# The down-projection of a two-layer decoder: eight groups of blocks in place of nine, the last bank copied ahead of the SiLU, other pages for the first group's operands

## The chip, the cores and the metric

The kernel runs on one core of one Trainium2 chip. The metric is the device time of one execution in microseconds (us); the time before is the median of three runs.

Five engines have queues of their own, and each runs its queue in order. TensorE (PE in the profile) multiplies matrices into PSUM. VectorE (DVE), ScalarE (ACT) and GpSimd (POOL) compute element by element. SyncE (SP) issues the DMA transfers between HBM and the on-chip memory SBUF. An instruction that waits holds back all that stand behind it in its own queue.

## The reference

Two layers, each a token mixer and then a feed-forward block (the ConvFFN), both followed by a LayerNorm over a scaled residual. The change lies in the feed-forward block of both layers (1024 tokens, width 1024, FFN_DIM 2816, that is 22 blocks of 128 channels):

```
def conv_ffn(h, w_up, b_up, conv_w, conv_b, w_down, b_down):
    up = causal_dwconv(h @ w_up + b_up, conv_w, conv_b)
    g, val = jnp.split(up, 2, axis=-1)
    return (jax.nn.silu(g) * val) @ w_down + b_down

# in each layer, with sh2, sc2, g2 worked out from the conditioning vector c
h = x * (1.0 + sc2) + sh2
y = conv_ffn(h, w_up[l], b_up[l], conv_f_w[l], conv_f_b[l], w_down[l], b_down[l])
x = layer_norm(DEEPNORM_ALPHA * x + (1.0 + g2) * y, ln_g[l, 1], ln_b[l, 1])
```

Everything is float32.

## The kernel before

**Products in three parts.** A float32 operand is split into a rounded high part (ScalarE's cast, L125) and the rest as a low part (a subtraction, L126). A product is three matmuls: high by high, high by low, low by high (L130 to L132 in the down-projection, L1092 to L1094 in the up-projection). Tiles of SBUF are "pages" of 128 partitions; a page can be written again when its last reader is done.

**Up-projection (`up_phase`).** One iteration for each of the 22 blocks of channels, and one more to finish. The seven products of a Strassen-like scheme go into PSUM banks called `upa`, `upb` and `upd`, are summed on VectorE (L1116), pass through the three-tap convolution (a ScalarE activation, L1125, and VectorE's L1129) into tiles `cv`, and through the SiLU (L1211). The finished block goes to memory as `d_act` (L1177). The value half of a block is convolved one iteration later than its gate half: the bank that the last product (number 4, into `upb`) fills is copied to `upc` by ScalarE at the head of the next iteration (L1151). TensorE, ScalarE and VectorE run this function in the order in which it is written.

**Down-projection (`ffn`, from L1244).** The 22 blocks are taken in groups of `sizes`, 2, 3, 3, 3, 3, 2, 2, 1, 3. For each block of a group `load_act` loads the activations from `d_act` (tile `actr`) and splits them, and `load_wdown` loads the rows of the weights (tile `wdn`), multiplies them by the gate row (L1240) and splits them. The parts go to pages named `dn`; `sets` are two sets of such pages that the groups use in turn, and the first group has a choice of its own: `ya`, pages of the up-projection's operand `A`, and `xc`.

Then `out_group` (L892) makes eight token tiles of 128 by 1024. Each gathers 6 n matmuls for n blocks in two banks of PSUM (tile `og`; there are three such pairs, and two more single banks, in place of the up-projection's eight). In the first group ScalarE copies the pair to the sum `r` (L903); in each later group VectorE adds it (L905).

**Work beside it.** After each group `pump` lets a few steps of two generators into the program. One (only in layer 0) works out the next layer's modulation: loads of `wada`, VectorE's L260. The other, `residual_in` (L1024), adds the residual to `r`: it loads two rows of parameters (`agab`), then for each of eight token tiles a tile `xr` of the residual (two buffers), multiplies it (L1034), adds (L1035) and adds it to `r` (L1036). What is left is done ahead of the last group's products.

At the end of layer 0 the last group goes through `boundary`: each token tile gets its LayerNorm (VectorE's L352, L354, L137, GpSimd's L138, VectorE's L363); then each half of the tokens is transposed on TensorE (L333, tile `tr`), taken out of PSUM by ScalarE (L340, L343) and VectorE (L346) as the next layer's operand `h`, from which the next projection (`prj`) starts. Beside it weights of the next layer are split (ScalarE's cast to `vwh`, GpSimd's subtraction to `vwl`). In front of the transposes TensorE has the matmuls of the modulation (`modp`, L269, and `gatet`, L286).

Outside `up_phase` a scheduler orders the instructions of each engine by estimated times and priorities, so a change of group sizes moves instructions at many places.

Of the kernel before, what the change touches and what calls it, by code (L numbers as in the profile page):

```python
# [13 lines left out]
F32R = mybir.dt.float32r  # L14
# [6 lines left out]
P = 128  # L21
D = 1024
S = 1024
L = 2
# [26 lines left out]
class Trunk:  # L51
# [1044 lines left out]
    def up_phase(self, l, H, A):  # L1096
        nc = self.nc
        act, v = nc.scalar, nc.vector
# [5 lines left out]
        cg, cv = self.page("Ra", "upc"), self.page("Ra", "upc")  # L1104
# [13 lines left out]
        def cast(n, src):  # L1118
            act.copy(self.up_w[n][:, 0], src)  # L1119

        def sub(n, src):
            tt(self.up_w[n][:, 1], src, self.up_w[n][:, 0].bitcast(F32), ALU.subtract)

        def lin(m, c, u):
            act.activation(out=u, in_=c, func=AF.Identity, bias=self.ffcc[:, m:m + 1], scale=self.ffw[:, 2, m:m + 1])  # L1125
# [7 lines left out]
        b, d = self.bank("upb"), self.bank("upd")  # L1133
# [4 lines left out]
        for f in range(NF + 1):  # L1138
            run, nxt = f < NF, f + 1 < NF
# [8 lines left out]
                a = self.bank("upa")  # L1148
                self.product(a, H, 2)
            if f:  # L1150
                act.copy(cv[:, 0:512], pb)  # L1151
                lin(NF + f - 1, cv, uv)
                if run:
                    cast(4, o22)
# [49 lines left out]
            taps(f, cg, ug)  # L1204
            self.product(b, H, 4, True)
            pb = b
            if nxt:
                b = nb
                act.copy(e1, b)
                sub(7, n21)  # L1210
# [33 lines left out]
    def ffn(self, l, H, A, O):  # L1244
        nc = self.nc
        self.ffn_cols(l)
        self.psum(0, 8)
        with self.tc.manual_schedule(engines={nc.tensor.engine, nc.scalar.engine, nc.vector.engine}):
            self.up_phase(l, H, A)
        self.psum(3, 2)  # L1250
        pages = lambda tag, n: [self.page(tag, "dn", F32R) for _ in range(n)]
        ya, xc = pages(A + "a", 8), pages(O + "c", 4)
        xa = []
        for _ in range(2):
            t = self.page(O + "a", "dn", F32R, (P, 4, 1024))
            xa += [t[:, i] for i in range(4)]
        yb, yc = pages(A + "b", 4), pages(A + "c", 4)
        sets = [(ya[:6], yc + ya[6:]), (xa[:6], xa[6:] + yb)]
        grow = self.gate_row(l, 1)
        r = {}  # L1260
        f0 = 0
        sizes = (2, 3, 3, 3, 3, 2, 2, 1, 3)
        for j, n in enumerate(sizes):
            last = j == len(sizes) - 1
            acts, wts = (ya[:4], xc) if j == 0 else sets[j % 2]
            lhs = [self.load_act(l, f0 + i, acts[2 * i], acts[2 * i + 1]) for i in range(n)]
            w = [self.load_wdown(l, f0 + i, wts[2 * i], wts[2 * i + 1], grow) for i in range(n)]
            f0 += n
            if j == 0:
                for t in (4, 5, 6, 7, 0, 1, 2, 3):  # L1270
                    r[t] = self.page("Ra" if t < 4 else "Rb", "r")
                self.out_group(lhs, w, r, None, (4, 5, 6, 7, 0, 1, 2, 3), True)
                self.bg.append(self.residual_in(l, r, O))
                if l + 1 < L:
                    self.mod_tile = [self.page(O + "c", "wada") for _ in range(3)] + [self.page(O + "c", "macc")]
                self.pump(2)
            elif not last:
                self.out_group(lhs, w, r)
                self.pump(3 * n + 2 if l + 1 < L else 2)
            else:  # L1280
                self.drain_bg()
                if l + 1 < L:
                    for ww in range(2):
                        self.affine_cols(l + 1, ww)
                    pre = self.za_first(l + 1, A)
                    Hn = self.boundary(l, 1, lhs, w, r, O)
                    self.bg.append(self.residual(l, r, "tmp"))
                    return Hn, pre
                self.final_rows(l, lhs, w, r)
# [143 lines left out]
```

## Time and profile before

| | us |
|---|---|
| median of three runs | 2542.33 |
| lowest and highest | 2537.85, 2546.43 |
| the profiled execution | 2538.86 |
| its span in the trace | 2537.2 |
| TensorE busy | 2354.1 (93%) |
| VectorE busy | 2066.2 (81%) |
| ScalarE busy | 1066.0 (42%) |
| GpSimd busy | 395.1 (16%) |

The profiled execution lies within the runs' range; its mean granted TensorE clock is 0.959 of full speed (2.4 GHz; 0.50 is 1.2 GHz). Times in the rows are us from the start of the span. In layer 0 the passage from up- to down-projection lies at 1000 to 1045 us and the down-projection ends at 1302; in layer 1 the passage lies at 2255 to 2297 and the down-projection ends at 2518. Busy shares are averages over stages with different limits, so each place is read by itself: first what TensorE waits for there, then what the engine named was doing.

### The profile page before, as it was taken

The page shows a single profiled execution, that of the slowest core. Times are in us where ns is not written, and L with a number is a line of the kernel's source. Part 1 is how long each engine was busy: PE and PEld are TensorE (multiplying, and loading weights), DVE is VectorE, ACT ScalarE, POOL GpSimd, SP SyncE. Part 2 cuts the span into 40 slices and gives each one's busy share as a digit, 9 for nine tenths or more (in the row PEclk, how much of TensorE's full clock was granted, in tenths as well). Part 3 has the DMA queues.
Part 4 walks back from the last instruction along what each step waited for, and adds up shares of the span by engine and source line. Part 5 has one row for each costly group of instructions (what it writes and reads, how often), then busy time and mean ns, then how long its engine had stood idle before and what let it go on. Part 6 is the DMA issues. An engine that isn't in the chain of part 4 may idle for free. (4 is left out here: it accounts for less than half of the span.)

```text
span 2537.2 us, 28532 instructions
## 1 busy us (share of the span) xinstructions
PE 2354.1 (93%) x10846; PEld 1912.6 (75%) x10846; DVE 2066.2 (81%) x2794; ACT 1066.0 (42%) x1708; POOL 395.1 (16%) x213
## 2 busy tenths in 40 slices
PE   8999989988999999999789999999899999989996
PEld 7777768766888887788578776777678888868885
DVE  7998787889887888778979987768887777797768
ACT  4314744645554554311131157445554554552111
POOL 1243160433000000000020542213510000000003
PEclk9998979999999999999889998999899999999998
DMA  8443433222332334645513244220322222254311
GB/s 295 152 153 130 160 142 117 75 100 71 112 110 90 117 108 155 206 142 182 172 61 133 87 160 164 95 108 32 108 75 83 84 83 83 84 183 148 100 42 67
DMA packets 88826, 302.47 MB, mean 119 GB/s; under 512 B 9392, under 2 KB 18928, under 8 KB 87152
## 3 DMA queue, kind: packets, MB, share of 16 engines
q1 hardware_dynamic: 88688, 300.65, 34.9%
q8 instruction: 85, 1.39, 0.2%
q14 instruction: 53, 0.43, 0.1%
HBM read 232.42 MB, written 68.19 MB: 118 GB/s over the span
## 5 line engine op out<-in xcount | busy, mean ns | idle before, releaser
L130 PE MATMUL og<-dn,dn 128*128 128x512 f32 x704 | 281.2, 399 | 37.6 <-DVE r L905 21.6
L1092 PE MATMUL upb<-comb,uw 128*128 128x512 f32 x704 | 275.9, 392 | 10.9 <-DVE upc L1116 6.7
L131 PE MATMUL og<-dn,dn 128*128 128x512 f32 x704 | 278.5, 396 | 0.0
L132 PE MATMUL og<-dn,dn 128*128 128x512 f32 x704 | 278.3, 395 | 0.0
L1093 PE MATMUL upb<-comb,uw 128*128 128x512 f32 x704 | 275.4, 391 | 2.7 <-DVE comb L980 2.7
L1094 PE MATMUL upb<-comb,uw 128*128 128x512 f32 x704 | 274.9, 391 | 0.0
L1116 DVE TENSOR_TENSOR uw<-wu,uw 128x512 fp32r<-128x512 f32 x210 | 144.2, 687 | 125.3 <-ACT uw L1119 125.3
L138 POOL TENSOR_TENSOR lnrs<-lnrs,mhalf 128x1 f32<-128x1 f32 x32 | 20.8, 653 | 1386.1 <-DVE lnrs L137 1374.4
L905 DVE TENSOR_TENSOR r<-og,r 128x1024 f32<-128x1024 f32 x144 | 174.6, 1219 | 66.8 <-PE og L132 66.0
L1129 DVE SCALAR_TENSOR_TENSOR cv<-upc,pc,cv 128x1023 f32<-128x1023 f32 (+1 forms) x176 | 225.4, 1281 | 2.8
L130 PEld LDWEIGHTS og<-dn,dn 128*128 128x128 f32 x704 | 134.5, 191 | 72.1 <-DVE r L905 27.2
L410 DVE SCALAR_TENSOR_TENSOR convacc<-convy,pc,convacc 128x1023 f32<-128x1023 f32 (+14 forms) x120 | 178.7, 1489 | 1.8
L125 ACT CAST dn<-actr 128x1024 fp32r<-128x1024 f32 x44 | 46.0, 1049 | 306.5 <-PE og L131 146.2
L1092 PEld LDWEIGHTS upb<-comb,uw 128*128 128x128 f32 x704 | 132.7, 188 | 41.6 <-DVE upc L1116 8.4
L1119 ACT CAST uw<-wu 128x512 fp32r<-128x512 f32 x210 | 121.7, 616 | 83.6 <-DVE wu L1116 77.1
L1093 PEld LDWEIGHTS upb<-comb,uw 128*128 128x128 f32 x704 | 132.8, 189 | 31.8 <-DVE comb L980 4.5
L132 PEld LDWEIGHTS og<-dn,dn 128*128 128x128 f32 x704 | 134.4, 191 | 28.2
L131 PEld LDWEIGHTS og<-dn,dn 128*128 128x128 f32 x704 | 134.8, 192 | 27.4
L1094 PEld LDWEIGHTS upb<-comb,uw 128*128 128x128 f32 x704 | 132.7, 189 | 27.6
L1093 PE MATMUL upd<-comb,uw 128*128 128x512 f32 x352 | 138.1, 392 | 5.9 <-DVE comb L980 5.9
L1092 PE MATMUL upd<-comb,uw 128*128 128x512 f32 x352 | 137.7, 391 | 0.0
L1094 PE MATMUL upd<-comb,uw 128*128 128x512 f32 x352 | 137.3, 390 | 0.0
(327 smaller groups left out, 5812.1 us busy)
## 6 DMA issues: line engine op xcount, KB each, us to landing
wada<-in_w_ada SPq DMA_DIRECT2D x96, 512.0 KB, 4.5
wu<-in_w_up_t SPq DMA_DIRECT2D x84, 512.0 KB, 3.6
d_act<-cv SPq DMA_DIRECT2D x44, 512.0 KB, 2.6
actr<-d_act SPq DMA_DIRECT2D x44, 512.0 KB, 4.2
wdn<-in_w_down SPq DMA_DIRECT2D x44, 512.0 KB, 4.2
win<-in_w_fm SPq DMA_DIRECT2D x24, 512.0 KB, 4.5
wtm<-in_w_tm SPq DMA_DIRECT2D x16, 512.0 KB, 3.7
d_v<-vhl SPq DMA_DIRECT2D x16, 512.0 KB, 2.9
```

What stands on the lines that cost most here:

```text
L125: nc.scalar.copy(hi, src)
L130: mm(ps, lh, rh, start=first, stop=False)
L131: mm(ps, lh, rl, start=False, stop=False)
L132: mm(ps, ll, rh, start=False, stop=last)
L410: nc.vector.scalar_tensor_tensor(out=acc[:, d:], in0=y[:, :S - d], scalar=w(30 - d), in1=acc[:, d:], op0=ALU.mult, op1=ALU.add)
L905: nc.vector.tensor_tensor(out=r[t], in0=ps, in1=r[t], op=ALU.add)
L1092: mm(ps, w[:, 0, ks], hi[k], start=k == 0 and not more, stop=False, skip_group_check=True)
L1093: mm(ps, w[:, 0, ks], lo[k], start=False, stop=False, skip_group_check=True)
L1094: mm(ps, w[:, 1, ks], hi[k], start=False, stop=k == 3, skip_group_check=True)
L1116: v.tensor_tensor(out=o, in0=x, in1=y, op=op)
L1119: act.copy(self.up_w[n][:, 0], src)
L1129: v.scalar_tensor_tensor(out=u[:, d:], in0=c[:, :S - d], scalar=self.ffw[:, 2 - d, m:m + 1], in1=u[:, d:], op0=ALU.mult, op1=ALU.add)
```

## The change

Four edits.

1. In the last up-projection iteration the copy of the last bank moves from the head of the finishing iteration to a place ahead of the SiLU (a new line, L1209, in place of L1151's last run).
2. The groups are 2, 3, 3, 3, 3, 3, 2, 3: eight in place of nine.
3. The first group's activations use two new pages (`xb`) that hold the up-projection's operands of products 5 and 6, and the second group takes the set with `ya`; the sets swap their turns.
4. In layer 0 `pump` lets in 3 n steps after a group of n blocks in place of 3 n + 2; in layer 1 nothing after the first group.

```
@@ up_phase
             if f:
-                act.copy(cv[:, 0:512], pb)
+                if run:
+                    act.copy(cv[:, 0:512], pb)
                 lin(NF + f - 1, cv, uv)
...
             self.product(b, H, 4, True)
             pb = b
+            if not nxt:
+                act.copy(cv[:, 0:512], pb)
             if nxt:
                 b = nb
                 act.copy(e1, b)
@@ ffn
-        sets = [(ya[:6], yc + ya[6:]), (xa[:6], xa[6:] + yb)]
+        xb = []
+        for _ in range(2):
+            t = self.page(O + "b", "dn", F32R, (P, 2, 1024))
+            xb += [t[:, i] for i in range(2)]
+        sets = [(xa[:6], xa[6:] + yb), (ya[:6], yc + ya[6:])]
...
-        sizes = (2, 3, 3, 3, 3, 2, 2, 1, 3)
+        sizes = (2, 3, 3, 3, 3, 3, 2, 3)
...
-            acts, wts = (ya[:4], xc) if j == 0 else sets[j % 2]
+            acts, wts = (xb, xc) if j == 0 else sets[j % 2]
...
-                self.pump(2)
+                    self.pump(2)
...
-                self.pump(3 * n + 2 if l + 1 < L else 2)
+                self.pump(3 * n if l + 1 < L else 2)
```

(The first `pump` moves into the branch for layer 0 by its indentation.)

Layer 0 has 55 background steps left at that point, 47 of the modulation and then 8 of the residual. Before, 2, 13, 24, 35, 46, 54 and 55 of them are in the program after each group, so that the residual is done ahead of the last two groups; now 2, 11, 20, 29, 38, 47 and 53, and the last two ahead of the last group.

Line numbers behind L1151 grow by one, behind L1209 by three, behind the sets by up to seven.

How the instructions move, at three places; `dn`, `actr`, `wdn`, `upc` and `og` are the tiles named above, with their buffer numbers.

ScalarE around the last copy of a bank, layer 1, before:

```order
L125 CAST dn_16524<-actr_16691 128x1024 [waits DMAHW0_49]
L125 CAST dn_16525<-actr_16695 128x1024 [waits DMAHW1_49]
L1211 ACTIVATE cv_13766<-cv_13766 128x1024 [waits DVE_49,Activation_49]
L1151 COPY upc_13764<-upb_16374 128x512 [waits PE_49]
L1125 ACTIVATE cv_13767<-upc_13764,ffcc_13744,pc_91 128x1024 [waits Activation_49]
L125 CAST dn_16530<-wdn_16894 128x1024 [waits DVE_49]
L125 CAST dn_16532<-wdn_16899 128x1024 [waits DVE_49]
L903 COPY r_16554<-og_16562 128x1024 [waits PE_49]
```

and now:

```order
L125 CAST dn_16500<-actr_16666 128x1024 [waits DMAHW5_49]
L125 CAST dn_16502<-actr_16670 128x1024 [waits DMAHW6_49]
L125 CAST dn_16504<-wdn_16684 128x1024
L1209 COPY upc_13750<-upb_16360 128x512 [waits PE_49,Activation_49]
L1214 ACTIVATE cv_13752<-cv_13752 128x1024 [waits DVE_49,Activation_49]
L1125 ACTIVATE cv_13753<-upc_13750,ffcc_13730,pc_91 128x1024 [waits Activation_49]
L125 CAST dn_16510<-actr_16862 128x1024 [waits DMAHW0_49]
L125 CAST dn_16511<-wdn_16874 128x1024
L125 CAST dn_16512<-wdn_16879 128x1024 [waits DVE_49]
L903 COPY r_16542<-og_16550 128x1024 [waits PE_49]
```

The copy now stands ahead of the SiLU, and one more cast of weights stands ahead of both; the first copy of `og` (L903) has a cast of a loaded `actr` in front of it.

VectorE around the add that frees the last product (`upc<-upe,upb`), layer 0, before:

```order
L1029 TENSOR_SCALAR agab_8855<-agab_8855 128x1024 [waits DMAHW4_49,PE_49]
L1116 TENSOR_TENSOR cv_4857<-cv_4857,cv_4859 128x1024 [waits DVE_49]
L1116 TENSOR_TENSOR upc_4855<-upe_4850,upd_7577 128x512 [waits PE_49,Activation_49]
L126 TENSOR_TENSOR dn_7677<-actr_7835,dn_7677 128x1024 [waits DMAHW6_49,Activation_49]
L1034 TENSOR_TENSOR xr_8856<-xr_8856,agab_8855 128x1024 [waits DMAHW7_49,DVE_49]
L1116 TENSOR_TENSOR upc_4856<-upe_4851,upb_7527 128x512 [waits PE_49]
L1034 TENSOR_TENSOR xr_8856<-xr_8856,agab_8855 128x1024 [waits DMAHW0_49]
L126 TENSOR_TENSOR dn_7678<-wdn_7847,dn_7678 128x1024 [waits Activation_49]
```

and now:

```order
L126 TENSOR_TENSOR dn_7687<-actr_7691,dn_7687 128x1024 [waits Activation_49]
L1116 TENSOR_TENSOR cv_4857<-cv_4857,cv_4859 128x1024 [waits DVE_49]
L126 TENSOR_TENSOR dn_7684<-wdn_7849,dn_7683 128x1024 [waits PE_49]
L126 TENSOR_TENSOR dn_7666<-actr_7837,dn_7665 128x1024 [waits DMAHW4_49,Activation_49]
L126 TENSOR_TENSOR dn_7688<-actr_7695,dn_7688 128x1024 [waits Activation_49]
L1116 TENSOR_TENSOR upc_4855<-upe_4850,upd_7577 128x512 [waits PE_49,Activation_49]
L1116 TENSOR_TENSOR upc_4856<-upe_4851,upb_7527 128x512 [waits PE_49]
L126 TENSOR_TENSOR dn_7686<-wdn_7854,dn_7685 128x1024 [waits Activation_49]
```

The residual's L1029 and L1034 are gone from here; four subtractions L126 stand ahead of the two bank adds.

TensorE at the end of layer 0's down-projection (`tr` are the transposes), before:

```order
L286 MATMUL gatet_8851<-ident,gatec_8691 16x128
L333 MATMUL tr_9268<-ident,r_7711 128x128
L333 MATMUL tr_9268<-ident,r_7712 128x128
L333 MATMUL tr_9268<-ident,r_7713 128x128
L132 MATMUL og_9369<-dn_7685,dn_7668 128x512
L130 MATMUL og_9369<-dn_7671,dn_7669 128x512
L131 MATMUL og_9369<-dn_7672,dn_7669 128x512
L333 MATMUL tr_9268<-ident,r_7714 128x128
L132 MATMUL og_9369<-dn_7671,dn_7670 128x512
```

and now:

```order
L132 MATMUL og_9413<-dn_7685,dn_7668 128x512
L130 MATMUL og_9413<-dn_7671,dn_7669 128x512
L131 MATMUL og_9413<-dn_7672,dn_7669 128x512
L132 MATMUL og_9413<-dn_7671,dn_7670 128x512
L269 MATMUL modp_8897<-ones,macc_7832 128x1 x8
L286 MATMUL gatet_8910<-ident,gatec_8693 16x128
L333 MATMUL tr_9254<-ident,r_7713 128x128
L333 MATMUL tr_9254<-ident,r_7714 128x128
L333 MATMUL tr_9254<-ident,r_7715 128x128
```

Before, transposes of the first token half lie among the last tiles' matmuls; now all of them follow the last tile, behind `gatet`. In VectorE's order between the last L905 of the fifth group and the last L363 there are now 25 L905 (33 before), 11 L126 (13), 2 L1240 (3), 17 L260 (16) and no L346 (7).

## Rows read from the trace of the kernel before

**Rows 1.** The page: busy us of each engine, share of the span, instructions.

```profile
PE 2354.1 (93%) x10846; PEld 1912.6 (75%) x10846; DVE 2066.2 (81%) x2794; ACT 1066.0 (42%) x1708; POOL 395.1 (16%) x213
```

**Rows 2.** TensorE's waits, 918 to 1320 us: us in total, times, longest.

```profile
PE og L130 <- DVE r L905: 19.7, 7, 9.9
PE upb L1092 <- DVE upc L1116: 4.7, 1, 4.7
PE og L130 <- ACT r L903: 4.2, 1, 4.2
...
PE tr L333 <- DVE r L363: 3.8, 2, 3.0
```

**Rows 3.** TensorE's waits, 2255 to 2500 us.

```profile
PE og L130 <- ACT upc L1151: 11.0, 1, 11.0
PE og L130 <- DVE r L905: 1.9, 3, 0.6
PE upb L1092 <- DVE upc L1116: 1.1, 1, 1.1
PE og L130 <- ACT r L903: 0.8, 1, 0.8
```

**Rows 4.** Windows: length, busy us (count) by engine, granted clock, DMA share, GB/s.

```profile
1010.00:1022.00 12.00, 11.39 (x38) 9.04 (x39) 12.00 (x12) 6.04 (x7) 0.00 (x0) 0.74 0.68 208
1024.50:1036.00 11.50, 7.28 (x24) 5.82 (x24) 9.36 (x13) 4.80 (x5) 0.00 (x0) 0.70 0.61 193
2274.70:2286.00 11.30, 11.22 (x40) 9.10 (x41) 10.41 (x11) 6.10 (x7) 0.00 (x0) 0.80 0.60 197
```

**Rows 5.** One window, tile og alone: layer 0's second group.

```profile
1044.80:1077.40 32.60, 32.60 (x145) 27.02 (x144) 8.49 (x7) 1.00 (x1) 1.00 0.63 214
```

**Rows 6.** VectorE's groups, 1181.5 to 1312.1 us: count, busy us, mean ns, idle.

```profile
L905 DVE TENSOR_TENSOR r<-og,r 128x1024 f32<-128x1024 f32 x33 | 40.0, 1219 | 1.5 <-PE og L132 1.4
...
L363 DVE TENSOR_SCALAR r<-r,lnmv,lnrs 128x1024 f32<-128x1024 f32 x8 | 10.1, 1263 | 1.0 <-POOL lnrs L138 0.9
```

**Rows 7.** ScalarE's timeline, layer 1: start, us, instruction, [idle before <- releaser].

```profile
2267.76 1.04 ACT L125 CAST dn<-actr 128x1024 fp32r<-128x1024 f32 x1 [1.75 <-DMA actr<-d_act]
2273.20 1.06 ACT L1211 ACTIVATE cv<-cv 128x1024 f32<-128x1024 f32 x1 [4.39 <-DVE cv L1116]
2274.16 0.57 ACT L1151 COPY upc<-upb 128x512 f32<-128x512 f32 x1
```

**Rows 8.** SyncE's queue (DMA issues), layer 1.

```profile
2261.59 1.73 SPq L1232 DMA_DIRECT2D actr<-d_act  x2
```

**Rows 9.** VectorE's timeline, layer 0.

```profile
1009.87 0.68 DVE L1116 TENSOR_TENSOR upc<-upe,upb 128x512 f32<-128x512 f32 x1
```

**Rows 10.** VectorE's timeline, layer 1.

```profile
2257.32 0.68 DVE L1116 TENSOR_TENSOR upc<-upe,upb 128x512 f32<-128x512 f32 x1
```

**Rows 11.** ScalarE's timeline, layer 0.

```profile
1006.52 1.04 ACT L125 CAST dn<-actr 128x1024 fp32r<-128x1024 f32 x1 [5.44 <-DMA actr<-d_act]
```

**Rows 12.** VectorE's timeline, the boundary of the layers.

```profile
1304.30 2.40 DVE L363 TENSOR_SCALAR r<-r,lnmv,lnrs 128x1024 f32<-128x1024 f32 x1
...
1309.16 2.92 DVE L363 TENSOR_SCALAR r<-r,lnmv,lnrs 128x1024 f32<-128x1024 f32 x1
```

**Rows 13.** ScalarE's timeline, the boundary: transposed banks taken out of PSUM.

```profile
1312.65 1.45 ACT L340 ACTIVATE hf<-tr,sh,sc 128x512 f32<-128x512 f32 x2 [1.97 <-PE tr L333]
...
1315.02 1.46 ACT L340 ACTIVATE hf<-tr,sh,sc 128x512 f32<-128x512 f32 x2
```

**Rows 14.** TensorE's timeline, the boundary: the next layer's first projection matmul.

```profile
1319.86 0.56 PE L130 MATMUL prj<-h,wh 128*128 128x512 f32 x1
```

**Rows 15.** GpSimd's timeline, the boundary.

```profile
1303.79 2.35 POOL L126 TENSOR_TENSOR vwl<-wtm,vwh 128x1024 fp32r<-128x1024 f32 x1
...
1309.19 5.10 POOL L126 TENSOR_TENSOR vwl<-wtm,vwh 128x1024 fp32r<-128x1024 f32 x2
```

**Rows 16.** Loads of tile xr, 1180 to 1310 us: issue to landing.

```profile
DMA to landing us min/median/max: 3.3/4.4/5.8
```

## The prediction

> **What bounds the kernel now.** I read the page first, then TensorE's waits in the two stretches that the change touches, then the clock there, then the timeline of the engine that each wait names, and last the groups of VectorE at the end of layer 0.
>
> TensorE is busy for 93% of the span [rows 1]. Only its idle time and its time at half clock can be had, and the question is how much of either lies in the two down-projections. The reader is to see three places.
>
> First, the passage from up- to down-projection. In layer 0 the last product waits 4.7 us for VectorE's add L1116 and the fourth output tile 4.2 us for ScalarE's copy L903 [rows 2]; in layer 1 the second output tile waits 11.0 us for the copy L1151, and 1.1 and 0.8 us are lost beside it [rows 3]. Each long wait has a price behind it: the mean granted clock is 0.74, 0.70 and 0.80 in the eleven or twelve us that follow, though TensorE is busy in nearly all of two of them [rows 4].
>
> Second, the end of layer 0's down-projection: seven waits for VectorE's add L905, 19.7 us, the longest 9.9, and 3.8 for its L363 [rows 2].
>
> Third, in layer 1 the group of one block: three waits for L905, 1.9 us [rows 3].
>
> Elsewhere in the down-projection TensorE is the bound: a group of three blocks has 144 matmuls and takes 32.6 us without a gap at full clock [rows 5], about 10.9 us a block. Its eight adds on VectorE need 8 x 1.22 = 9.8 us, however many blocks there are [rows 6]. A group of one block therefore leaves VectorE almost nothing for other work.
>
> **The change, part by part.** The profiled execution took 2538.9 us, the median of the three runs is 2542.3; gains are worked out in the first and taken off the second.
>
> *Copy of the last bank.* In layer 1 it starts at 2274.16, right behind the SiLU of 2273.20, which had waited 4.39 us for VectorE; the last cast in front of the SiLU starts at 2267.76, itself behind a load [rows 7]. In ScalarE's new order the copy stands behind the casts and ahead of the SiLU. With the casts as they are it would start at 2268.8. They move too: two of their loads went out at 2261.59 [rows 8], when VectorE had ended the first tile's subtraction. The residual's four loads no longer stand around the first tile's load, so I let the two go out some 2.9 us earlier and the third cast end at 2265.9. One more cast of 1.05 follows: copy at 2267.3, end near 2267.9. The ends are 2265 (no wait for loads) and 2270 (loads as before, one cast more).
>
> *Operands on other pages, residual later.* Ahead of the add that frees the last product, VectorE loses the residual's instructions and gains subtractions of the first group, since their pages come free later. For layer 0 I walked VectorE's new order with 1.22 us for a subtraction and 0.68 for a bank add: the add of 1009.87 [rows 9] ends near 1008.3, and the wait is about 2.5 instead of 4.7 us. In layer 1 the same add, at 2257.32 now [rows 10], ends near 2259.4: 1.45 us later, a loss. The bounds are waits of 1 and 5.5 us, for a subtraction ahead of the add needs a cast of a loaded tile, and that cast had ScalarE idle for 5.44 us [rows 11].
>
> *Layer 0's passage.* Now 4.7 + 4.2 us are idle, and half clock costs 0.26 x 12 = 3.1 in the first stretch and, its idle part left out, about 1.8 in the second: 13.8. After: 2.5 for the product and 1.2 for the fourth tile, whose copy L903 stands behind one cast that waits for a load; and 0 to 1.5 us of half clock, which I let lie between none (a gap of 1 us) and the 3.1 behind a gap of 4.7. Gain 8.6 to 10.1, taken as **9**; by the bounds 4 to 12.
>
> *Layer 1's passage.* Now 12.9 us idle and 0.20 x 11.3 = 2.3 at half clock, 15.2. After: 2.5 for the product, some 2.3 between the first tile and the second, 0.6 at the fourth, and 2 to 3 of half clock: 8. Gain **7**, by the bounds 3 to 11.
>
> *Eight groups for nine.* One pass of adds less in each layer; TensorE's work stays (22 blocks of 48 matmuls). At the end of layer 0 I counted VectorE's orders between the fifth group's last add and the last L363: 25 L905 in place of 33 (9.8 us by [rows 6]), two subtractions and one L1240 less (they move ahead, 3.7), seven L346 less (they move behind the end, some 0.6 each, 4.2), one background step more (1.3). That is 16.4; since instructions overlap a little, 15.5. The last L363 starts at 1309.16 and takes 2.92 [rows 12], so it ends at 1312.1; 15.5 less is 1296.6. Two more corrections: the stretch now holds some 8 us of waits and slowed instructions (the two L363 of [rows 12] take 2.40 and 2.92, the other six of the eight that sum to 10.1 [rows 6] 0.8 each), of which I let half go; and VectorE enters it about 1 us earlier, as the groups in front carry two background steps fewer. So 1291, with 1286 and 1297 as the ends. What gets worse: all eight residual additions now fall into the last two groups, and all 64 transposes stand behind the last output tile, so that the tiles no longer hide the first half's: 16 banks at 2.37 us a pair [rows 13], 19 us from about 3 us ahead of the end of the last L363. The next layer's first matmul would start at 1307, in place of 1319.86 [rows 14]: **13**; with the ends 7 and 18.
>
> In this trace the two long L363 lie beside GpSimd's subtractions of 1303.79 and 1309.19 [rows 12, 15]. Here a rule of the Trainium skill speaks against the change: "SBUF — State Buffer", section "Who interferes with whom", says that VectorE and GpSimd share one pair of ports under an exclusive lock, and that an instruction of VectorE with two operands in SBUF, or in a two-port mode, and one of GpSimd that reads SBUF hold each other out for a whole instruction. By that rule the residual's instructions, which have two operands in SBUF and now stand where GpSimd's subtractions run, can be held too; if each of the four subtractions held VectorE for its full 2.35 us, 9.4 in place of the 3.7 lost now, the end would come up to 6 us later and the time be about 2517. No row here shows a residual instruction beside a subtraction of GpSimd; I leave the sum as it is.
>
> *Layer 1's group of one block.* Its 1.9 us go: **2**.
>
> The sum is 9 + 7 + 13 + 2 = 31: 2507.9 in the profiled execution, **2511** against the median.
>
> **Rivals.** *A: the passages only rename their wait.* ScalarE's queue still holds three casts of loaded tiles ahead of the copy, and L903 stands behind more of them. For it: such casts left ScalarE idle for 1.75 and 5.44 us [rows 7, 11]. Against: the SiLU's own wait, 4.39, is gone from in front of the copy in any case. Were 16 to become 3: 2511 + 13 = 2524.
>
> *B: the end of layer 0 gives nothing.* VectorE stays full, now with the residual, and the tail of 19 us eats the rest. For it: the residual's share in the last two groups grows. Against: 9.8 us of adds are really gone. 2511 + 13 = 2524.
>
> *C: both, or the change does not do what it says,* since loads that stay where they are decide the waits: 2537 to 2542.
>
> *D: slower, by loads of the residual.* VectorE's queue is in order and the residual's tiles come through two buffers, so a pair of loads can start only when the pair before is used. With all four pairs in the last two groups an L1034 that waits for its load stops the output adds behind it, and TensorE behind those. If a pair waited w us, 4 w is lost. From w = 7.8 on the gain of 31 is gone; at w = 10 the time is 2551. For it: these loads take 3.3 to 5.8 us to land [rows 16], and other loads are issued ahead of them. Against: VectorE has some nine instructions between the use of a pair and the next, about 10 us, longer than a load.
>
> **How the numbers follow.** The main case has 0.62, with its own range 2499 to 2523 (the terms' ends do not all fall together). A has 0.16, B 0.10, C 0.06, D 0.06. What a measurement of this kernel can tell from no change is about 0.3%, 7.6 us. Faster by more: main, A and B: 0.88. Within: C and the near side of D: 0.07. Slower: the rest of D, 0.05. The range 2497 to 2534 takes in the main case, A and B; above it lie C and D, a little over one in ten, and below it somewhat less.
>
> **What would show it.** Right: in layer 1 the copy at 2266 to 2269 and no wait of TensorE for it over 4 us; the waits for L905 at layer 0's end down from 19.7 to under 5, with an idle stretch of 15 us or more ahead of the 64 transposes, and the first projection matmul 7 to 18 us earlier against the start of the sixth group; a mean granted clock above 0.85 behind the passages' gaps. Wrong: the copy later than 2271, a wait for L903 over 4 us, VectorE waiting for loads ahead of L1034 in the last two groups, or half clock for over 5 us behind the short gaps.

## The result, and the profile after

The changed kernel takes 2516.95 us (median of 4 runs, 2512.38 to 2519.65) against 2541.22 for the kernel before beside it: a ratio of 0.9901, 95% interval 0.9878 to 0.9924. Measured a second time, unchanged and beside new runs of the kernel before, it took 2513.65 against 2543.6: 0.988, interval 0.9863 to 0.9897. The gain is 24 us in the one, 30 in the other; the forecast was 31, at 2511 in a range of 2497 to 2534.

The page's first line answers to [rows 1]: TensorE's busy time is almost the same, its span is 21.7 us shorter.

```profile
PE 2349.1 (93%) x10846; PEld 1913.0 (76%) x10846; DVE 2045.7 (81%) x2778; ACT 1063.6 (42%) x1708; POOL 395.4 (16%) x213
```

TensorE's waits in layer 0, 918 to 1320 us (us in total, times, longest), which answer to [rows 2]:

```profile
PE gatet L286 <- DVE gatec L283: 22.0, 1, 22.0
...
PE upb L1092 <- ACT upe L1185: 1.9, 1, 1.9
PE og L130 <- ACT r L903: 1.1, 1, 1.1
PE upb L1092 <- DVE upc L1116: 0.8, 1, 0.8
```

The seven waits for L905 are gone. In their place stands one idle stretch of 22.0 us in front of the transposes. In the passage there are waits of 1.9, 0.8 and 1.1 us where there were 4.7 and 4.2; the first of them is a new one, of the product before the last, for a copy of ScalarE (L1185). In layer 1, 2230 to 2500 us, two waits are left of the four of [rows 3]:

```profile
PE og L130 <- ACT upc L1209: 2.8, 1, 2.8
PE upb L1092 <- DVE upc L1116: 2.8, 1, 2.8
```

Windows around the passages' gaps (length, busy us of PE, PEld, DVE, ACT and POOL with counts, granted clock, DMA share, GB/s) answer to [rows 4]. The clock there is 0.86, 1.00 and 0.85 where it was 0.74, 0.70 and 0.80. The third window, unlike the one of [rows 4], holds the wait for the copy itself, 2.8 us, so TensorE is busy for only 8.6 us of it:

```profile
1010.00:1022.00 12.00, 10.39 (x37) 8.01 (x38) 11.02 (x12) 6.29 (x8) 0.00 (x0) 0.86 0.69 224
1024.50:1036.00 11.50, 10.45 (x46) 8.18 (x45) 11.45 (x14) 11.33 (x12) 0.00 (x0) 1.00 0.64 199
2254.60:2266.00 11.40, 8.64 (x32) 6.96 (x32) 10.56 (x12) 11.07 (x12) 0.00 (x0) 0.85 0.66 221
```

ScalarE's timeline in layer 1 (start, us, instruction, idle before it and releaser) answers to [rows 7]:

```profile
2254.86 1.04 ACT L125 CAST dn<-actr 128x1024 fp32r<-128x1024 f32 x1 [2.26 <-DMA actr<-d_act]
2255.81 1.04 ACT L125 CAST dn<-wdn 128x1024 fp32r<-128x1024 f32 x1
2256.76 0.58 ACT L1209 COPY upc<-upb 128x512 f32<-128x512 f32 x1
2257.24 1.06 ACT L1214 ACTIVATE cv<-cv 128x1024 f32<-128x1024 f32 x1
```

The copy starts right behind the casts, and the SiLU behind it waits for nothing. To compare the two clocks I take the last matmul of the up-projection into the bank `upa`, which starts 10.85 us earlier than before; with that added, the copy stands at 2267.6 on the clock of the kernel before, where 2274.16 was and 2267.3 was forecast.

By stages, each from one landmark of TensorE to the next, in us (`upa`: its last matmul; "second" and "sixth": first matmul of that many-th group, or of the same block of 128 channels where the groups differ; `prj`, `sc`, `upd`: first matmul of the next layer's projections, of a layer's attention, and of its up-projection). "After" is the changed kernel's first profile, "again" its second:

| stage | before | after | again |
|---|---|---|---|
| layer 0, attention, `sc` to `upd` | 287.7 | 292.5 | 287.1 |
| layer 0, passage, `upa` to second group | 50.0 | 41.9 | 41.4 |
| layer 0, second to sixth group | 134.4 | 134.5 | 134.5 |
| layer 0, end, sixth group to `prj` | 140.8 | 133.5 | 133.4 |
| layer 1, `prj` to `sc` | 228.8 | 229.6 | 231.0 |
| layer 1, attention, `sc` to `upd` | 281.8 | 279.7 | 279.7 |
| layer 1, passage | 51.3 | 43.3 | 43.0 |
| layer 1, second group to the last matmul | 220.5 | 217.8 | 217.8 |

So the change gained 8.1 and 8.0 us in the passages, 7.3 at layer 0's end, 2.7 with the group of one block, and 2.1 in layer 1's attention, and lost 0.8 between: 27.4. The first row has the same instructions in the same order in all three and still differs by 5.4. A stage can therefore differ by that much from one execution to the next without a change in the program, and in the changed kernel's first profile this went 4.8 us against it.

Why layer 0's end gave 7.3 and not 13 is seen on VectorE. Its timeline there, with the last two LayerNorms (L363) at the end:

```profile
1269.53 2.38 DVE L363 TENSOR_SCALAR r<-r,lnmv,lnrs 128x1024 f32<-128x1024 f32 x1
...
1272.96 2.23 DVE L1035 TENSOR_TENSOR xr<-xr,agab 128x1024 f32<-128x1024 f32 x1
...
1276.36 2.73 DVE L363 TENSOR_SCALAR r<-r,lnmv,lnrs 128x1024 f32<-128x1024 f32 x1
...
1284.01 3.37 DVE L1036 TENSOR_TENSOR r<-r,xr 128x1024 f32<-128x1024 f32 x1
...
1294.12 1.70 DVE L363 TENSOR_SCALAR r<-r,lnmv,lnrs 128x1024 f32<-128x1024 f32 x2 [0.23 <-POOL lnrs L138]
```

and GpSimd's beside it:

```profile
1269.01 5.09 POOL L126 TENSOR_TENSOR vwl<-wtm,vwh 128x1024 fp32r<-128x1024 f32 x2
1276.20 2.34 POOL L126 TENSOR_TENSOR vwl<-wtm,vwh 128x1024 fp32r<-128x1024 f32 x1 [2.10 <-ACT vwh L125]
...
1283.93 2.36 POOL L126 TENSOR_TENSOR vwl<-wtm,vwh 128x1024 fp32r<-128x1024 f32 x1
```

Each slowed instruction of VectorE lies beside one of GpSimd's four subtractions and ends 0.5 to 1.1 us behind its end. The four take 10.7 us where at the usual 0.8 (L363) and 1.2 us (L1035, L1036) they would take 4.0: 6.7 us lost, against 3.7 in [rows 12]. L1035 and L1036 are the residual's. Counted from the start of the sixth group, the last L363 ends at 119.1 us where it ended at 133.1: 14.0 us earlier, while 21 were forecast. TensorE's end of it, with the row that answers to [rows 14]:

```profile
1292.20 0.38 PE L286 MATMUL gatet<-ident,gatec 128*16 128x128 f32 x1 [21.99 <-DVE gatec L283]
...
1310.27 0.78 PE L130 MATMUL prj<-h,wh 128*128 128x512 f32 x1
```

### The profile page after: what moved, and what is told of

It reads as the page before. It is cut to its first block, busy times and chain, and to the rows that moved or that the text cites. A ratio compares the mean times of both kernels' runs of the same rounds, so it can differ in the third digit from the quotient of the medians.

```text
span 2515.5 us, 28512 instructions
## 1 busy us (share of the span) xinstructions
PE 2349.1 (93%) x10846; PEld 1913.0 (76%) x10846; DVE 2045.7 (81%) x2778; ACT 1063.6 (42%) x1708; POOL 395.4 (16%) x213
## 5 line engine op out<-in xcount | busy, mean ns | idle before, releaser
L130 PE MATMUL og<-dn,dn 128*128 128x512 f32 x704 | 275.9, 392 | 4.4 <-ACT upc L1209 2.8
L131 PE MATMUL og<-dn,dn 128*128 128x512 f32 x704 | 275.2, 391 | 0.0
L132 PE MATMUL og<-dn,dn 128*128 128x512 f32 x704 | 274.8, 390 | 0.0
L138 POOL TENSOR_TENSOR lnrs<-lnrs,mhalf 128x1 f32<-128x1 f32 x32 | 21.7, 683 | 1351.7 <-DVE lnrs L137 1348.1
L905 DVE TENSOR_TENSOR r<-og,r 128x1024 f32<-128x1024 f32 x128 | 155.6, 1217 | 59.7 <-PE og L132 59.0
L130 PEld LDWEIGHTS og<-dn,dn 128*128 128x128 f32 x704 | 132.5, 188 | 33.1 <-ACT upc L1209 3.2
L132 PEld LDWEIGHTS og<-dn,dn 128*128 128x128 f32 x704 | 132.6, 188 | 27.6
L131 PEld LDWEIGHTS og<-dn,dn 128*128 128x128 f32 x704 | 132.5, 188 | 27.1
```

The costliest lines, as they stand in the source:

```text
L130: mm(ps, lh, rh, start=first, stop=False)
L131: mm(ps, lh, rl, start=False, stop=False)
L132: mm(ps, ll, rh, start=False, stop=last)
L905: nc.vector.tensor_tensor(out=r[t], in0=ps, in1=r[t], op=ALU.add)
```

## The experiments

Each version was timed against the kernel before on its own chip, so versions are compared by their ratios, with the 95% interval in brackets. The stages of its profile, as in the table above, say where the time went; "passages" are those of layer 0 and layer 1, in this order, "the end" is layer 0's, "the attention" layer 1's.

**The copy alone.** The kernel before with the first edit only.

```
@@ up_phase, kernel before
             if f:
+                if run:
                     act.copy(cv[:, 0:512], pb)
...
             pb = b
+            if not nxt:
+                act.copy(cv[:, 0:512], pb)
```

> The kernel before with the first edit alone: the last bank's copy ahead of the SiLU, all else as before (nine groups, old pages, old pump). Theory (a stall in a queue that either edit can undo): in ScalarE's order of this version the copy stands ahead of two casts of loaded tiles as well, and the first L903 right behind it, so layer 1's second tile waits about 1 us in place of 11.0 and its half clock (2.3) goes, and in layer 0 the 4.2 us before the fourth tile shrink below 1.5 with 1.8 of half clock; the product's wait of 4.7 in layer 0 stays. Gain 13 to 17 us against the kernel before, about 2526. Rival 1 (the new pages are needed, the copy alone only skips the SiLU's 5.4 us): gain 5 to 6, about 2535. Rival 2 (the copy only changes the name of the wait): gain under 3. Layer 0's end as before in all.

Measured 0.9934 (0.9922 to 0.9947), 2527.42. The passages take 43.5 and 38.3 us, 6.5 and 13.0 less than before; layer 0's end takes 142.5, no better. In layer 1 the copy stands ahead of two casts that wait for loads:

```profile
2263.95 1.98 ACT L125 CAST dn<-wdn 128x1024 fp32r<-128x1024 f32 x2
2265.84 0.57 ACT L1209 COPY upc<-upb 128x512 f32<-128x512 f32 x1
2266.61 1.05 ACT L125 CAST dn<-actr 128x1024 fp32r<-128x1024 f32 x1 [0.20 <-DMA actr<-d_act]
2269.66 1.05 ACT L125 CAST dn<-actr 128x1024 fp32r<-128x1024 f32 x1 [1.99 <-DMA actr<-d_act]
```

This is as the theory had it: the copy's new place alone takes more from layer 1's passage than all four edits together (8.0).

**All but the copy.** The changed kernel with that edit undone (the same lines, the other way).

> The changed kernel with the first edit undone: the copy again behind the SiLU. Theory: with the residual's instructions out of VectorE's queue the SiLU no longer waits long (none in layer 1, 1.2 us in layer 0 in the changed kernel's trace), so the copy comes 1 us later in layer 1 and about 2.8 in layer 0; 3 to 5 us slower than the changed kernel, about 2521. Rival (the copy's place carries the passage's gain of layer 1): 8 to 11 us slower, about 2527, with a wait of the second tile of 9 us or more in layer 1.

Measured 0.9924 (0.9912 to 0.9937), 2526.82. The passages take 49.5 and 44.4, the end 131.4, the attention 285.2. Layer 1's passage loses 1.1 against the changed kernel, as expected. Layer 0's loses 7.6, more than the 2.8, for its fourth tile now waits longer for L903. With that and an attention 5.5 us longer the time is that of the rival, but not for the rival's reason: in layer 1 the second tile waits 2.2 us, not 9.

```profile
PE og L130 <- ACT r L903: 5.8, 1, 5.8
...
PE upb L1092 <- ACT upe L1184: 1.8, 1, 1.8
```

So in layer 1 the stall goes with the copy's edit alone, and also with the other three edits without it, and the gains do not add: 13.0 and 6.9 apart, 8.0 together. Which of the three does it was not tried. In layer 0 the gain is the copy's.

**GpSimd's work later.** The splits of the next layer's value weights (cast and subtraction) are held until the boundary is over.

```
@@ proj_tm, changed kernel
-            self.split(hi, lo, raw)
+            with self.tc.issue_after(<last bank out of PSUM>):   # layer 1 only
+                self.split(hi, lo, raw)
```

> The changed kernel with the next layer's four splits for the value projection (cast vwh, GpSimd's subtraction vwl) held until the last transposed bank of the boundary is out of PSUM. Theory (VectorE and GpSimd exclude each other): the four slowed instructions at layer 0's end (L363 2.38 and 2.73, L1035 2.23, L1036 3.37 us, 6.7 above their usual length) fall back to 0.8 and 1.2, the last L363 ends some 6 to 7 us earlier against the start of the sixth group, and the run takes about 2511. Rival 1 (those four are slow for another reason, such as the loads beside them): no change, 2517. Rival 2 (the value projection's operands come too late then): slower than the changed kernel, with TensorE waiting for vwl.

Measured 0.9915 (0.99 to 0.9931), 2521.45. Layer 0's end takes 126.8 us, 6.7 less than in the changed kernel. VectorE's groups of 1180 to 1287 us (count, busy us, mean ns):

```profile
L1040 DVE TENSOR_TENSOR r<-r,xr 128x1024 f32<-128x1024 f32 x8 | 9.7, 1208 | 0.0
...
L1039 DVE TENSOR_TENSOR xr<-xr,agab 128x1024 f32<-128x1024 f32 x6 | 7.2, 1202 | 0.0
L363 DVE TENSOR_SCALAR r<-r,lnmv,lnrs 128x1024 f32<-128x1024 f32 x8 | 6.3, 794 | 0.3 <-POOL lnrs L138 0.2
```

L1040 and L1039 are what L1036 and L1035 are in the changed kernel. No instruction is slow any more (L363 had a mean of 1241 ns in the changed kernel), so rival 1 falls. But `prj` to `sc` takes 238.5 in place of 229.6, and the attention 287.6. TensorE waits 7.2 us in the value projection for VectorE's `convy`, which stands in its queue behind a split of 3.31 us and a wait for a load of 4.70. So rival 2 came true as well.

**The gate row earlier.**

```
-            later = self.mods(1, (1, 0, 2, 3, 4, 5))
+            later = self.mods(1, (1, 0, 2, 5, 3, 4))
```

> The changed kernel with another order of the modulation's parts (the gate row ahead of the shift and scale of the feed-forward block), so that the transposes of the first token half do not stand behind the gate row's TensorE matmul, which waits for VectorE. Theory: the first half's 32 transposes start when tile 3 is normalised, 3 to 5 us earlier, and their removal from PSUM lies beside the last tiles' LayerNorm; the first projection matmul comes 2 to 5 us earlier: about 2514. Rival (VectorE's queue is full, and the eight L346 that then fall into it, 0.6 us each, push the last L363 back by as much): 0 to 1 us, 2517.

Measured 0.9916 (0.9902 to 0.993), 2524.5. The transposes start at 1276.9, 105.1 us from the sixth group in place of 115.7, and yet the end takes 135.8, 2.3 more. The expectation missed; the rival had the direction, with 0 to 1 us less in place of 2.3 more. The rest of the loss is the attention, 286.9 us. TensorE now waits within the transposes, for VectorE's L260 and L363 among others:

```profile
1276.44 0.59 PE L269 MATMUL modp<-ones,macc 128*128 128x1 f32 x2 [5.92 <-DVE macc L260]
...
1292.67 1.79 PE L333 MATMUL tr<-ident,r 128*128 128x128 f32 x8 [2.58 <-ACT hf L340]
...
1299.07 0.69 PE L333 MATMUL tr<-ident,r 128*128 128x128 f32 x2 [1.93 <-DVE r L363]
```

**The four subtractions on VectorE.**

```
@@ proj_tm, changed kernel, layer 1 only
+                nc.scalar.copy(hi, raw)
+                with self.tc.issue_after(<last L363>):
+                    nc.vector.tensor_tensor(out=lo, in0=raw, in1=hi.bitcast(F32), op=ALU.subtract)
```

> The changed kernel with the four subtractions for the next layer's value projection moved from GpSimd to VectorE and held until the boundary's last L363 is issued; their casts stay where they are. Theory (the lock, and not the casts or the loads): no GpSimd subtraction is left beside VectorE at layer 0's end, so the first projection matmul comes 7 to 9 us earlier against the last product of the up-projection, as with the whole split held (8.4); and since the input pages come free 10 to 15 us earlier than there, the 7 us that TensorE then lost in the value projection shrink to 0 to 3. About 2511 to 2514, or 4 to 8 below the changed kernel on the same chip. Rival (what the boundary gains is lost again in the value projection whatever engine does the subtraction): as the changed kernel.

Measured 0.9907 (0.989 to 0.9925), 2519.63: 6 us more than the changed kernel beside it (2513.65), where 4 to 8 less were expected. No instruction of VectorE is slow here either, though ScalarE's four casts stay in the stage, and the last L363 ends 112.2 us behind the sixth group's start in place of 119.1. The end takes only 3.4 less (130.1, not 7 to 9 less), since three of the casts now stand among the copies by which ScalarE takes the transposed banks out of PSUM; `prj` to `sc` takes 227.1 (2.5 less). But the attention takes 290.5 in place of 279.7. The gain was made where it was expected, though half as large, and lost again in a stage that no edit touched.

**Casts behind the copy.** What the copy waits for in the changed kernel.

```
@@ load_act, changed kernel
+        if f in (3, 4):
+            with self.tc.issue_after(<the last copy>):
+                self.split(hi, lo, raw, self.nc.vector)
```

> The changed kernel with the casts of the second group's second and third block (the ones that wait for loads) held behind the last bank's copy. Theory (in the changed kernel these casts took the place of the SiLU as what the copy waits for): layer 1's second tile waits under 0.7 us in place of 2.8 and the half clock behind it (0.15 of 11.4 us) goes; layer 0 changes by under 2 us. 3 to 5 us below the changed kernel on the same chip. Rival (the casts held then make the second group late): no gain, with TensorE waiting at the second group's first tiles.

Measured 0.9875 (0.9854 to 0.9896), 2512.03, 1.6 under the changed kernel beside it, short of the 3 to 5 that were expected; the runs overlap. The passages take 40.9 and 40.2 (0.5 and 2.8 less than in the run beside it). No wait for the copy is left in layer 1, but one of 1.3 us for L903 has come. Part of the 2.8 is the clock: over the 6 us behind layer 1's wait of 2.75 us for the last product it is 1.00 here, while the next run has 0.50 behind the same wait.

**Both of these together.**

> Both of the above together: the changed kernel with the four subtractions on VectorE behind the last L363, and the two casts behind the copy. They lie at different places, so the gains add: 7 to 13 us below the changed kernel on the same chip, about 2506 to 2510. Rival: no more than the better of the two alone.

Measured 0.9895 (0.9876 to 0.9914), 2516.6, 3 us above the changed kernel beside it, not 7 to 13 below. The end (130.1) and `prj` to `sc` (227.9) kept their gains; layer 1's passage took 41.5, and the attention 289.2. And the changed kernel once more, as the measure beside the three:

> The changed kernel once more, unchanged, as the measure for the three beside it on this chip: 0.990 of the kernel before, within 0.002.

0.988, within what was expected.

**Ten groups.**

```
-        sizes = (2, 3, 3, 3, 3, 3, 2, 3)
+        sizes = (2, 3, 3, 3, 3, 2, 1, 1, 1, 3)
```

> The changed kernel with ten groups (2, 3, 3, 3, 3, 2, 1, 1, 1, 3) in place of eight: two more passes of eight adds a layer, and three groups of one block in a row. Theory (each pass costs VectorE's 9.8 us where VectorE is full, and a group of one block costs TensorE about 2.8 us, as nine groups do against eight in layer 1): in layer 1 about 8 us more after the passage (2.8 for each group of one block); at layer 0's end between 16 and 20 us more; the passages as in the changed kernel. In all 24 to 28 us slower than the changed kernel, 2537 to 2542. Rival (the number of passes does not matter, what the change gained at layer 0's end came with the residual's new place): under 10 us slower.

Measured 1.0029 (1.0019 to 1.0038), 2548.74. Layer 1 from the second group takes 226.4, 8.6 more: 2.9 for each group of one block. Layer 0's end takes 149.9, 16.4 more for two passes of adds. Both came as expected, and the rival falls. The attention takes 15 us more (294.9), which puts the whole above the 24 to 28 us. TensorE's waits in layer 0:

```profile
PE og L130 <- DVE r L905: 17.7, 15, 2.8
PE gatet L286 <- DVE gatec L283: 9.3, 1, 9.3
```

**The whole second group behind the copy**, alone and with the subtractions on VectorE (the condition becomes `f in (2, 3, 4)`).

> As the version with two casts held behind the copy, but all three activation blocks of the second group held (cast and subtraction). Theory (in that version the subtraction of the first one still stands ahead of the add that frees the last product): the product's wait in layer 1 falls from 2.8 to about 1 us, in layer 0 the two waits of 1.4 and 1.6 to under 1 in sum; both passages together 2 to 5 us shorter than with two casts held, the second group not late. 2508 to 2511, 0.986 of the kernel before. Rival (the add waits for TensorE and the first group's own subtractions, not for this one): no change, 0.9875.

> The same, with the four subtractions of the value projection on VectorE behind the last L363. Theory: layer 0's end and the start of the next layer's projections gain 3.4 and 2.5 us as in the run with these alone, but there the granted clock of layer 1's attention was lower (0.88 against 0.92) and the stage 10.8 us longer; if that came with the order of the instructions it comes again, and this version is about 5 us slower than the one beside it, 2513 to 2516. Rival (the attention's clock varies by chance from one run to the next): 4 to 7 us faster than the one beside it.

Measured 0.99 (0.9887 to 0.9914), 2515.84, and 0.9876 (0.9861 to 0.9891), 2508.75. In both the passages are the shortest of all, 39.0 and 37.5 in the first, 39.2 and 37.5 in the second; the product's wait in layer 1 fell to 1.6 only, not to 1. Both have an attention of 288.9, which takes the gain back: by its ratio the first is no faster than the changed kernel, and the second is where the changed kernel was in its better measurement. The theory on the two side by side failed (the second is 7 us faster, as the rival said), but not for the rival's reason: the attention is long in both alike.

**The same order.** The last run puts the attention to the test: two changes that leave the order of its instructions as it is in the changed kernel.

> The version with two casts held behind the copy, and in it the four splits for the value projection held until the boundary's last bank but one is out of PSUM; chosen because the order of TensorE's instructions is the changed kernel's throughout, and every other engine's in layer 1's attention. Theory 1 (the lock with GpSimd): layer 0's end takes 126 to 128 us from the sixth group's start to the first projection matmul, against 133.5. Theory 2 (the length of layer 1's attention goes with the order of its instructions: 279.7, 279.7 and 279.8 us in the three runs that share one order, 283.8 to 294.9 in the seven with others): 279.5 to 280.5 us here. Rival to 2 (its clock varies by chance): between 283 and 291. The stretch behind the boundary may lose 0 to 9 us (it lost 8.9 where the splits were held one bank longer, in another order). In all 2503 to 2514; with no loss there, 0.985 of the kernel before.

Measured 0.988 (0.986 to 0.99), 2512.8. Layer 0's end takes 126.8, as theory 1 had it, and the attention 279.6, as theory 2 had it. (The runs with other orders are nine, not seven, and the kernel before is a tenth, with 281.8.) One window over layer 1's attention, of this version, of the changed kernel and of the version with the whole second group held:

```profile
1533.60:1813.20 279.60, 249.21 (x1313) 195.14 (x1313) 213.90 (x346) 150.54 (x351) 80.51 (x46) 0.92 0.29 102
```

```profile
1539.90:1819.60 279.70, 249.28 (x1313) 195.12 (x1313) 213.84 (x346) 150.40 (x351) 80.45 (x46) 0.92 0.29 102
```

```profile
1533.80:1822.70 288.90, 255.21 (x1314) 199.25 (x1313) 217.36 (x347) 150.38 (x352) 79.82 (x46) 0.89 0.28 99
```

The clock is 0.92 in the two that have the changed kernel's order and 0.89 in the third, where TensorE is busy 6.0 us longer with the same work and idle for the other 3 us. The traces also show where most of it is lost. For the first 150 us of the stage the changed kernel and the third version agree to 0.3 us. Then come the 10 us from 160 to 170 us, first in the changed kernel, then in the third version:

```profile
1699.90:1709.90 10.00, 9.27 (x63) 7.52 (x62) 8.41 (x14) 6.51 (x21) 6.85 (x4) 0.93 0.24 79
```

```profile
1693.80:1703.80 10.00, 9.31 (x41) 7.30 (x41) 8.92 (x10) 3.04 (x8) 9.65 (x4) 0.58 0.28 91
```

TensorE is busy for as long in both, but at a clock of 0.58 it gets through 41 matmuls in place of 63. `prj` to `sc` lost 8.3 in the last run (237.9), so this version is no faster than the changed one either. No version here is clearly faster than the changed kernel: the three lowest medians (2508.75, 2512.03 and 2512.8) have ratios of 0.9875 to 0.988, within the interval of its second measurement.

## Why the prediction was right or wrong

**Passages: right, in size and in most of the mechanism.** 9 and 7 us were forecast; 8.1 and 8.0 came (8.6 and 8.4 in the second profile). The copy was forecast for 2267.3 (2267.6 came), the product's wait in layer 1 for 2.5 (2.8), the fourth tile's in layer 0 for 1.2 (1.1), and layer 1's two loads went out 2.5 us earlier (2.9).

Layer 0's product came out by luck. 2.5 us was forecast for the last product, behind VectorE's add; it waited 0.8. The other 1.9 were waited by the product before it, for ScalarE's copy L1185, behind two casts that had waited for a load:

```profile
1008.30 1.99 ACT L125 CAST dn<-actr 128x1024 fp32r<-128x1024 f32 x2 [3.51 <-DMA actr<-d_act]
1010.20 0.58 ACT L1185 COPY upe<-upb 128x512 f32<-128x512 f32 x1
```

The prediction weighed such casts for the last copy, for L903 and, in its bounds, for the last product, but not for this copy.

One reason given was not the deciding one: "the SiLU's own wait, 4.39, is gone from in front of the copy in any case" credits the copy's new place, but with the other three edits alone the SiLU waits for nothing in layer 1 either. The edits take the same wait away, and together they cost layer 1 5.0 us against the copy alone: 2.0 in the product's wait (2.8 against 0.8), 1.4 in the wait for the copy (2.8 against 1.3, now behind casts of loads), and most of the rest at half clock behind it. Rival A is there in part: a wait was renamed, from the SiLU's to a cast's. Of the signs named for being right only one is missed, and narrowly: the clock of the third window is 0.85, not above it.

**Layer 0's end: the right direction, the size wrong by half.** 13 (7 to 18) was forecast, 7.3 came. A pass of adds did cost about what was said (two passes more took 16.4 us, with 9.8 us of adds in each), the last output tile was followed by an idle TensorE, and the transposes took 17.9 us to the first projection matmul where 19 was said. The step that failed is the term of the waits and slowed instructions: "the stretch now holds some 8 us of waits and slowed instructions [...] of which I let half go". They did not go down by 4. The slowed part went up by 3.0, from 3.7 to 6.7, and VectorE still waited 5.0 (2.0 for the modulation's matmuls, 1.6 for a load, 1.1 and 0.2 beside), as much as before (4.9). These 4 and 3.0 are the 7 us by which the last L363 missed its forecast (14.0 us earlier in place of 21). With the subtractions held out of the stage it takes 126.8, 14.0 less than before. In all five versions that took the subtractions away from there, by holding them or by giving them to VectorE, the last L363 ended 112.2 to 113.0 us behind the sixth group's start, against 119.1 in the changed kernel.

That is the rule that the prediction weighed and left out of the sum. By the Trainium skill's "SBUF — State Buffer", section "Who interferes with whom", an instruction of VectorE with two operands in SBUF contends with one of GpSimd that reads SBUF. Here a residual instruction beside a subtraction took 3.37 us in place of 1.2, and all of the extra time went when GpSimd's work did: the trace agrees with the rule. The prediction's estimate from it was an end up to 6 us later and 2517; the slowed instructions cost 3.0 more than before, and 2516.95 and 2513.65 came. That the first lies so near to 2517 is luck, for layer 0's attention alone moved by 5 us between the two profiles. No residual instruction stood beside a subtraction in the trace before, as the prediction says, but another instruction with two operands in SBUF did, behind the last L363, and took 2.83 us in place of 0.7:

```profile
1312.00 2.83 DVE L346 TENSOR_TENSOR h<-hf,h 128x512 fp32r<-128x512 f32 x1
```

That row would have been a reason to put the rule into the sum.

**The group of one block:** 2 forecast, 2.7 came, and 2.9 for each in the run with three.

**What the prediction left out.** Layer 1's attention went from 281.8 to 279.7 without an edit of its own, and the projections in front of it lost 0.8 to 2.1. A sum over the edits alone could not have these. So the 30 us of the second measurement, so near to the 31, are in part luck: the passages and the group of one block gave their share, the end 5.7 less than its share, and the spans of the two profiled executions differ by 25 us, not by 30.

**Rivals.** B and C fell: the end gave 7.3 us and the whole 24 to 30. D fell: no L1034 waited for its load at layer 0's end in the changed kernel, and TensorE waited for L905 not at all.

**Open.** Why another order of the attention's instructions makes it longer stays open. Four profiles of one order took 279.6 to 279.8 us, ten of other orders, no two alike, 281.8 to 294.9. That ties the length to the order, and most of the loss that was followed up lies in a stretch at a lower clock; it does not say what in the order brings the clock down. Each other order was profiled once. Giving the subtractions to VectorE kept both layer 0's end and the value projection short (130.1 and 227.1), but each time with a slow order of the attention; a version that has both was not tried.

## What to carry to other kernels

Before adding up edits ask whether they take away the same wait: here four edits together gave one passage 8.0 us, and one of them alone 13.0. Where a full VectorE sets the end of a stage, list what GpSimd does in that stretch before work with two operands in SBUF is moved into it. And where a scheduler orders the instructions, compare the order in the stages that no edit touches; in this kernel one of them differed by up to 15 us, more than most of the edits.

## What the runs showed that was not expected

Layer 1's attention kept its length to 0.2 us in four profiles of one order of its instructions, and took between 281.8 and 294.9 us in other orders, with a granted clock of 0.92 at 279.6 and of 0.89 at 288.9. Layer 0's attention, whose order is the same in all of these, still spread over 287.0 to 292.5, so one order doesn't always mean one length. One and the same wait of 2.75 us of TensorE was followed by a clock of 1.00 in one run and of 0.50 in another, over 6 us. And starting the transposes 10.6 us earlier made the stage 2.3 us longer: TensorE, and the copies behind it, then waited for VectorE's L260 and L363 just where VectorE is full.
